# A sliding-window copy: two pairs of windows and three small DMAs placed among the software ring's DMAs

## The chip, the cores and the metric

The kernel runs on one core of a Trainium2 chip. A core has five engines that execute instructions (here only three of them issue anything: SP, ACT and POOL) and 16 DMA engines that move bytes between the chip's memory (HBM) and the core's on-chip memory (SBUF), or from HBM to HBM. The time is the device time of one execution in microseconds (us). Before the change the median of 3 runs was 743.77 us (742.8 to 744.65).

## The reference

```python
batch, length, dim = (32, 4096, 256)      # x, float32
window_size = 64; stride = 32
n_windows = (length - window_size) // stride + 1      # 127
for i in range(n_windows):
    start = i * stride
    result[:, i] = x[:, start:start + window_size].copy()
```

Nothing is computed. For each of 32 batches the output holds 127 windows of 64 rows of 256 numbers. A window is 64 KB; two neighbours overlap by half, so each block of 32 rows (32 KB) of the input goes to two windows, once as a second half and once as a first half.

## The kernel before, in words

The kernel only issues DMAs, on three queues, and no data passes through a compute engine.

- ACT's queue (the staged batches, lines 49 to 123): 11 of the 32 batches, 1, 4, 7 and so on up to 31, are loaded into SBUF (128 blocks of 32 KB, one to a partition) and stored from there twice, once as first halves and once as second halves. There are six buffers, and a semaphore `stored0` to `stored5` for each of them counts the stores.
- SP's queue (the direct batches, lines 175 to 190): the other 21 batches are copied from HBM to HBM, 16 windows at a time. Some of these are split into the two halves of the windows. The variables `turns` and `share` choose how the two hardware queues are paced against each other.
- POOL's queue (lines 192 to 201): the rest of the direct batches. POOL's DMAs are written by software into a ring of descriptors, which is why its queue is called the software ring here. It waits for the semaphore `near`, which the last but one 16-window copy of SP raises, and then issues 20 copies of 15 windows each (the list `edges`, one for each direct batch but the last). Before each copy it waits until the staged batches next to it have been stored. Then come one copy of 4 windows of batch 30 (`last`), its windows 112 to 115, and one copy `columns` of the nine windows 116 to 124.

`windows` (line 29) issues a copy of n windows of 64 KB. In the instruction each window is one row of two pieces of 32 KB, so its form is n x 2 x 8192 elements. `columns` (line 40) cuts each window into 16 parts of 4 KB and makes the part the outer count, so its form is 16 x n x 1024. SP issues the last two windows of batch 30 in the same way at line 203, when the last staged batch has been stored; then it waits for all semaphores at line 206. POOL issues `drain` (line 201) after its last copy.

Of the kernel before, what the change touches and what calls it, by code (L numbers as in the profile page):

```python
# [11 lines left out]
class Copier:  # L12
# [7 lines left out]
        self.nb = L // S  # L20
        self.nw = n_win

    def xap(self, block, dims):
        return bass.AP(self.x.tensor, self.x.offset + block * self.blk, dims)

    def oap(self, half_window, dims):
        return bass.AP(self.out.tensor, self.out.offset + half_window * self.blk, dims)

    def windows(self, q, b, w0, n, half=None, piece=DIRECT):

# [9 lines left out]
    def columns(self, q, b, w0, n):  # L40

        part = self.blk // 8
        row = [1, part]
        return q.dma_start(  # L44
            out=self.oap((b * self.nw + w0) * 2, [[part, 16], [2 * self.blk, n], row]),
            in_=self.xap(b * self.nb + w0, [[part, 16], [self.blk, n], row]),
        )

    def load(self, q, t, b, c, rows):
# [76 lines left out]
@with_exitstack  # L126
def kernel(
    ctx: ExitStack,
    tc: tile.TileContext,
    x: bass.AP,  # L130
    window_size: bass.AP,
    stride: bass.AP,
    out: bass.AP,
):
    nc = tc.nc
    W, S = int(window_size), int(stride)
    B, L, D = x.shape
    n_win = (L - W) // S + 1
    assert out.shape == (B, n_win, W, D)
    c = Copier(x, out, B, L, D, W, S, n_win)  # L140


    staged = [*range(1, B, 3)]
    items = [(b, -1 if b == B - 1 else 0, c.nb) for b in staged]
    place = {b: g for g, (b, _, n) in enumerate(items) if n == c.nb}
    direct = [b for b in range(B) if b not in staged]
    pool = ctx.enter_context(tc.tile_pool(name="xb", bufs=1))
    st = Staging(c, tc, pool, x.dtype, items, 6)
    ring_d, ring_s, ring_r = nc.sync, nc.scalar, nc.gpsimd
    done = tc.alloc_semaphore("done")  # L150
    near = tc.alloc_semaphore("near")
    rest = tc.alloc_semaphore("rest")
    total = {done: 0, near: 0, rest: 0}

    def count(dma, sem):
        dma.then_inc(sem, 16)
        total[sem] += 16

    sixteens = []
    for b in direct:
        w = 15 if b - 1 in staged else 0
        sixteens += [(b, w + 16 * j) for j in range((c.nw - w) // 16)]
    singles = [(B - 1, c.nw - 1, 1)]
    edges = [(b, 0 if b - 1 in staged else 112, 15) for b in direct[:-1]]
    last = B - 2
    edges.append((last, 112, 4))

    first_loads, loads, stores = 6 * 17, 5 * 17, 6 * 34  # L170
    turns = share = 0
    with tc.tile_critical():  # L172
        st.run(ring_s)

        for i, (b, w) in enumerate(sixteens):
            sem = near if i == len(sixteens) - 2 else done
            second = turns - first_loads - stores
            loading = turns < first_loads or 0 <= second < loads
            share += 120 if turns < 16 or -8 <= second < 16 else 90 if loading else 18
            if share >= 120:  # L180
                share -= 120
                turns += 4
                count(c.windows(ring_d, b, w, 16, 0), done)
                count(c.windows(ring_d, b, w, 16, 1), sem)
            else:
                turns += 3
                count(c.windows(ring_d, b, w, 16), sem)
            if i == len(sixteens) // 2:
                for b, w, half in singles:
                    count(c.windows(ring_d, b, w, 1, half, 2048), done)  # L190

        ring_r.wait_ge(near, 16)
        for b, w, n in edges:
            for k in (b - 1, b + 1):
                if k in place and b != last:
                    st.wait_stored(ring_r, place[k])
            count(c.windows(ring_r, b, w, n), rest)


        count(c.columns(ring_r, last, 116, 9), rest)  # L200
        ring_r.drain()  # L201
        st.wait_stored(ring_d, place[B - 1])
        count(c.columns(ring_d, last, 125, 2), done)
        total[st.ended] = st.count[st.ended]
        for sem, n in total.items():
            ring_d.wait_ge(sem, n)
# [35 lines left out]
```

## Time and profile before

| | |
|---|---|
| median of 3 runs | 743.77 us (742.8 to 744.65) |
| the profiled execution | 743.86 us |
| its span, first to last instruction | 742.1 us |
| SP's queue (q1) | 8016 packets, 154.32 MB |
| ACT's queue (q10) | 9104 packets, 138.41 MB |
| POOL's queue (q0) | 1168 packets, 20.51 MB |
| POOL starts its copies at | 649.11 us |
| POOL waits for a store from, for | 659.36 us, 36.49 us |
| POOL's last copy is issued at | 697.85 us |
| SP's last copy is issued at | 723.77 us |

The page gives the busy share of the 16 DMA engines in 40 slices of the span, the bytes that each of them moved, and the DMA queues by their packets. Another view gives the same shares in any stretch of the span, and one more follows the chain of waits that ended last. The trace also holds a record of each packet, with its start, its duration, its queue and its size, though not with the DMA engine that moved it.

### The profile page before, as it was taken

What the parts mean: (1) busy time and instruction counts of PE and PEld (TensorE: products, weight loads), DVE (VectorE), ACT (ScalarE), POOL (GpSimd) and SP (SyncE); (2) the same over time, 40 slices, a digit from 0 to 9 for tenths busy, and PEclk for the clock granted to TensorE, in tenths of its full rate; (3) what the DMA queues carried; (4) which work ended last, traced back from release to release, by engine and by line L of the source; (5) the groups of instructions that cost most, each with busy time, mean ns of one, the idle gap of its engine ahead of it and who ended that gap; (6) DMA issues with size and microseconds to landing.
All of it is one profiled execution on the core that took longest, in us unless ns stands there. A gap on an engine that the chain in (4) does not pass through costs nothing.

```text
span 742.1 us, 323 instructions
## 1 busy us (share of the span) xinstructions
POOL 12.7 (2%) x26
## 2 busy tenths in 40 slices
POOL 0000000000000000000000000000000000050100
DMA  8999999999999999999999999999999999999996
GB/s 361 424 430 427 435 431 428 423 435 425 428 427 426 428 428 420 429 435 427 427 427 412 433 435 431 427 436 432 434 424 429 430 424 426 428 435 432 421 420 253
DMA packets 18290, 313.26 MB, mean 422 GB/s; under 512 B 4336, under 2 KB 4336, under 8 KB 4528
## 3 DMA queue, kind: packets, MB, share of 16 engines
q1 hardware_dynamic: 8016, 154.32, 48.8%
q10 hardware_dynamic: 9104, 138.41, 44.0%
q0 software_dynamic: 1168, 20.51, 6.6%
q14 instruction: 2, 0.02, 0.0%
HBM read 220.95 MB, written 267.09 MB: 658 GB/s over the span
## 4 chain that ended last, share of the span: by engine, by line
another core or an unknown queue 92%; POOL 2%; issue 0%; POOLq 0%; SPq 0%
POOL out_dram L34 2%; POOLq L201 0%; POOLq L237 0%; SPq L172 0%; POOLq L114 0%
## 5 line engine op out<-in xcount | busy, mean ns | idle before, releaser
L34 POOL DMA_DIRECT2D out_dram<-in_x_dram x21 | 12.0, 575 | 685.4 <-DMA out_dram<-in_x_dram 648.7
L44 POOL DMA_DIRECT2D out_dram<-in_x_dram x1 | 0.6, 581 | 0.0
L223 POOL MEMSET const-float32-0.0<- 128x1 f32 x1 | 0.1, 98 | 0.2 <-issue 0.2
L223 POOL MEMSET const-bfloat16-1.0<- 128x1 bf16 x1 | 0.1, 101 | 0.0
L223 POOL MEMSET const-float32-1.0<- 128x1 f32 x1 | 0.1, 98 | 0.0
L223 POOL MEMSET const-uint8-127<- 128x1 uint8 x1 | 0.1, 98 | 0.0
## 6 DMA issues: line engine op xcount, KB each, us to landing
out_dram<-in_x_dram SPq DMA_DIRECT2D x92, 1024.0 KB, 99.8
out_dram<-xb ACTq DMA_DIRECT2D x21, 4096.0 KB, 138.5
out_dram<-in_x_dram SPq DMA_DIRECT2D x110, 512.0 KB, 90.2
xb<-in_x_dram ACTq DMA_DIRECT2D x10, 4096.0 KB, 130.5
out_dram<-in_x_dram POOLq DMA_DIRECT2D x20, 960.0 KB, 37.9
xb<-in_x_dram ACTq DMA_DIRECT2D x4, 1024.0 KB, 15.7
out_dram<-xb ACTq DMA_DIRECT2D x2, 1024.0 KB, 110.5
out_dram<-xb ACTq DMA_DIRECT2D x4, 512.0 KB, 94.4
```

Source lines behind the costliest of these rows:

```text
L34: return q.dma_start(out=self.oap((b * self.nw + w0) * 2 + h, [[2 * blk, n], row]), in_=self.xap(b * self.nb + w0 + h, [[blk, n], row]), m ...
L44: return q.dma_start(out=self.oap((b * self.nw + w0) * 2, [[part, 16], [2 * self.blk, n], row]), in_=self.xap(b * self.nb + w0, [[part, 16 ...
L223: nc = _bacc.Bacc("TRN2", target_bir_lowering=False, num_devices=1)
```

## The change

The software ring issues 26 DMAs instead of 22. The 4-window copy of batch 30 becomes two copies of 2 windows, one before the 17th of the 15-window copies and one before the 20th. Behind each of them stands a small new DMA, `pieces`: window 116 of the same batch is cut into 64 parts of 1 KB, and the even ones of these are copied, 6 parts by the first small DMA (`first` 0, `n` 3, two parts for each count of n) and 26 parts by the second (`first` 3, `n` 13). The last `columns` copy has eight windows instead of nine, and a new DMA `odd` behind it copies the 32 odd parts of window 116. The words by which the change was described say that its DMAs are reordered with four small ones between them so that one certain DMA engine gets one row of 64 KB less and another one more. What SP and ACT issue stays the same.

```diff
+    def pieces(self, q, b, w, first, n):
+
+        part = self.blk // 32
+        dims = [[4 * part, n], [2 * part, 2], [1, part]]
+        return q.dma_start(
+            out=self.oap((b * self.nw + w) * 2, dims, first * 4 * part),
+            in_=self.xap(b * self.nb + w, dims, first * 4 * part),
+        )
+
+    def odd(self, q, b, w):
+
+        part = self.blk // 32
+        dims = [[2 * part, 32], [1, part]]
+        return q.dma_start(
+            out=self.oap((b * self.nw + w) * 2, dims, part),
+            in_=self.xap(b * self.nb + w, dims, part),
+        )
...
     last = B - 2
-    edges.append((last, 112, 4))
...
         ring_r.wait_ge(near, 16)
-        for b, w, n in edges:
+        row = 116
+        for i, (b, w, n) in enumerate(edges):
+            if i == 16:
+                count(c.windows(ring_r, last, 112, 2), rest)
+                count(c.pieces(ring_r, last, row, 0, 3), rest)
+            if i == 19:
+                count(c.windows(ring_r, last, 114, 2), rest)
+                count(c.pieces(ring_r, last, row, 3, 13), rest)
             for k in (b - 1, b + 1):
-                if k in place and b != last:
+                if k in place:
                     st.wait_stored(ring_r, place[k])
             count(c.windows(ring_r, b, w, n), rest)
 
 
-        count(c.columns(ring_r, last, 116, 9), rest)
+        count(c.columns(ring_r, last, row + 1, 8), rest)
+        count(c.odd(ring_r, last, row), rest)
         ring_r.drain()
```

`xap` and `oap` get an argument `extra`, an offset in elements, that the new functions use. `self.blk` is 8192 elements, so `part` is 256 elements, 1 KB.

More of the change, by code (lines that the diff above doesn't have):

```diff
@@ L21, in __init__, with xap, oap @@
         self.nw = n_win
[L23 to L27, printed above, removed]
+    def xap(self, block, dims, extra=0):
+        return bass.AP(self.x.tensor, self.x.offset + block * self.blk + extra, dims)
+    def oap(self, half_window, dims, extra=0):
+        return bass.AP(self.out.tensor, self.out.offset + half_window * self.blk + extra, dims)
     def windows(self, q, b, w0, n, half=None, piece=DIRECT):
```

## The prediction

> **What bounds the kernel now.** I read the page first, then short windows at the end of the span, then the waits of SP's queue, then the packet records of the trace. The page:
>
> ```profile
> span 742.1 us, 323 instructions
> ...
> DMA  8999999999999999999999999999999999999996
> GB/s 361 424 430 427 435 431 428 423 435 425 428 427 426 428 428 420 429 435 427 427 427 412 433 435 431 427 436 432 434 424 429 430 424 426 428 435 432 421 420 253
> ...
> q1 hardware_dynamic: 8016, 154.32, 48.8%
> q10 hardware_dynamic: 9104, 138.41, 44.0%
> q0 software_dynamic: 1168, 20.51, 6.6%
> ...
> out_dram<-in_x_dram POOLq DMA_DIRECT2D x20, 960.0 KB, 37.9
> ...
> out_dram<-in_x_dram POOLq DMA_DIRECT2D x1, 576.0 KB, 42.3
> out_dram<-in_x_dram POOLq DMA_DIRECT2D x1, 256.0 KB, 38.0
> ```
>
> The reader is to see that nothing computes, that the 16 DMA engines are busy in every slice but the first and the last, and that the software ring (q0, 22 DMAs issued by POOL) carries only 20.51 of 313.26 MB. So the bytes set the time, and the only slack left is how evenly the 16 engines end. One microsecond at a time, with the columns stretch, its length, POOL, clock, DMA share and GB/s:
>
> ```profile
> 733.00:734.00 1.00, 0.00 (x0) 1.00 0.83 340
> 734.00:735.00 1.00, 0.00 (x0) 1.00 0.73 299
> 735.00:736.00 1.00, 0.00 (x0) 1.00 0.41 168
> 736.00:737.00 1.00, 0.00 (x0) 1.00 0.11 45
> 737.00:738.00 1.00, 0.00 (x0) 1.00 0.07 29
> 738.00:739.00 1.00, 0.00 (x0) 1.00 0.06 25
> 739.00:740.00 1.00, 0.00 (x0) 1.00 0.04 16
> ```
>
> A share of 0.06 is one engine in sixteen. From 737 to past 739 one engine works alone. SP waits for exactly that:
>
> ```profile
> SPq L206 <- DMA out_dram<-in_x_dram: 15.8, 1, 15.8
> ```
>
> The packet records give start, duration, queue and bytes, but no engine. On one engine a packet starts 3 to 6 ns before the last one's end, and the order of sizes on each queue is known from the program, so the 18,288 packets of the three data queues fall into 16 sequences of 19.578 MB each, all of them saturated from 2.8 us on (the latest one has 0.30 us of gaps). In the software queue each sequence has 38 packets of 32 KB, that is 19 rows of 64 KB, and 9 of 4 KB. Every 15-window DMA leaves out exactly one sequence, each a different one for 16 DMAs, and DMAs 17 to 20 leave out again the first four; those four get the rows of the 4-window DMA. So the ring deals rows in turn and goes on where the last DMA stopped: 20 x 15 + 4 = 304 = 16 x 19. I number the engines by it: the first DMA leaves out engine 15, the next 14, and so on. Where each engine's last packet ends, us from the span's start:
>
> ```
> engine   0      1      2      3      4      5      6      7
> end   735.77 734.14 734.86 735.20 739.70 734.26 735.11 734.94
> engine   8      9     10     11     12     13     14     15
> end   736.09 735.16 734.61 735.91 736.15 735.27 735.57 737.23
> ```
>
> Engine 4 ends 2.47 us after the next one. Its packets are only a little slower (16 KB: 622 ns on average against 615 to 620), and its lag behind the median engine, in bytes at 27 GB/s (32 KB in 1213 ns), grows through the whole span: 1.0 us at 69, 2.0 at 429, 3.3 at 609. After 739.70 comes the last count at 740.14 and the close until 742.09, 2.39 us together. The profiled execution took 743.86 us, 1.76 beyond its span and 0.09 above the median of 743.77.
>
> **What the change would be worth if the deal moved as described.** After 16 DMAs of 15 windows all engines have 15 rows and the next share is engine 0's. Two rows go to engines 0 and 1. A small DMA then moves the place by p, three 15-window DMAs follow, two rows, a small DMA that moves it by q, and the last 15-window DMA. With p = 3 and q = 13 the three DMAs leave out 4, 3 and 2, the two rows go to 2 and 3, the last leaves out 0: engine 4 has 18 rows, engine 1 has 20, the others 19. A row is two packets of 1245 ns on engine 4: 2.49 us, less two overlaps of 4 ns, 2.48. Engine 4 would end at 737.2, engine 1 at 734.14 + 2.48 = 736.6, and engine 15, untouched, at 737.2. Gain 2.4.
>
> **Why I don't take it.** The small DMA is written as n pieces of two steps, 3 x 2 x 256 elements, but the second step is 512 elements and the first 1024, so the two steps are one: the built program carries 6 x 256 and 26 x 256, with one counting step. A DMA that deals by its outer count has 6 and 26 to deal, never 3 and 13. The software ring of before has no copy with one counting step (its forms are 15 x 2, 4 x 2 and 16 x 9), so what the ring does with 6 and 26 has to be bounded:
> - It spreads them over all engines and does not move the place (p = q = 0): the 15-window DMAs leave out 1, 0, 15 and 0, the pairs go to 0, 1 and 15, 0. Sum: every engine 19 rows.
> - It moves by 6 and by 26, that is 10: engine 7 has 18, engine 1 has 20.
> - It moves by 6 and by 13, the largest count up to 16 that divides 26: engines 3 and 7 have 18, 0 and 1 have 20; engine 0 ends at 738.3.
>
> In all three engine 4 keeps its 19 rows and ends last. I take the first, because the hardware ring's one-step form, 16 x 8192, falls on all 16 engines in the records; but the sum is the same in each.
>
> The Trainium skill (DMA: Bandwidth & Descriptors, Why a DMA increments its semaphore by 16 and not by 1) says that the share count is the largest number up to 16 that divides the slowest counting step, but that the software ring gives some direct copies all 16 engines, and that the place moves only for fewer than 16. The 15 and 4 shares of this trace agree with its first half; no row here shows the exception. By the rule it would be 6 and 13, by the exception no move: 743.9 by either.
>
> **The rest of the change, on engine 4.** One 4 KB packet less: its group takes 159 ns, 156 from start to start. The window 116 comes instead as 64 pieces of 1 KB, 4 to an engine on average; I take 5 on engine 4. None of that size is in the trace; the 16 packets of 2 KB took 84 ns each, the 4-byte ones 9. A line through 84 and 159 gives 46 ns: 5 x 46 = 0.23 us, with ends 5 x 9 and 6 x 84, 0.05 to 0.50. Four more DMAs add a 4-byte packet each, three where the engine has no data (as its records show for the DMA that leaves it out), 6 ns from start to start: 0.02 to 0.07. Sum: -0.16 + 0.23 + 0.04 = +0.1, ends -0.1 and +0.4.
>
> **Off the path.** POOL issues 26 DMAs instead of 22, 575 to 581 ns each: 2.3 us more in all. The chain of waits has its last stretch
>
> ```profile
> 649.11 10.25 POOL out_dram L34 x18
> 659.36 36.49 another core or an unknown queue
> 695.85 0.28 issue
> 696.14 1.72 POOL out_dram L34 x3
> 697.85 0.58 POOLq L201
> ```
>
> The first pair and its pieces go ahead of the 36.5 us wait, the second pair, its pieces and the odd pieces behind it, so the last issue moves from 697.85 to at most 700.2. At 697.85 every engine still has 8 to 9 rows of 64 KB queued, and the first packet of the 4 KB columns starts at 732.74: more than 30 us of cover. If it were gone, each issue would cost its 0.58 us. No wait is added; the same 20 DMAs wait for the same stores, in the same order, and SP and ACT issue what they did. That two rows come earlier on engines 0 and 1 changes no end, since all are saturated. The close could grow with the number of DMAs that POOL drains: 26/22 of the 1.95 us after the last count would be +0.35, and I take nothing.
>
> Sum: 743.77 + 0.1 = **743.9 us**.
>
> **Rivals.**
> - *The place moves by 3 and 13 after all.* For: engine 4 is the one that ends last and engine 1 the one that ends first, so the numbers fit this trace exactly. Against: the instruction carries 6 and 26. Time: 743.77 - 2.48 + 0.1 = 741.4; engine 15 at 737.2 holds it from going lower.
> - *Slower: the place is carried from one execution to the next.* Before, 304 shares bring it back to where it began. With moves of 6 and 13 the sum is 323, 3 beyond 320, so each execution begins 3 engines on, and the pair of engines with 20 rows walks around. It decides where the pair holds engine 4 (2 executions in 16): 739.70 + 2.48 + 0.1 = 742.3, time 746.3. On engine 15 it would give 739.8, nothing. For: the place survives from DMA to DMA. Against: it needs the division rule, and then a bad place in most of the timed runs.
> - *Nothing is late for long:* engine 4's lag is this execution's alone. Then neither relief nor load shows, and the time lies within the runs' spread of 742.8 to 744.65.
>
> **Chances.** Within 0.3%, 2.2 us, is about what a measurement of this kernel can tell from no change. Engine 4 keeps 19 rows, with no extra row on it: 0.64, and its own range is 742.6 to 745.2 (the -0.1 and +0.75 of the bounds beside the runs' 0.9). Moved by 3 and 13: 0.24; its 2.4 us is just over the bound, so I count 0.14 of it as faster. Slower by carrying: 0.06. Something not named: 0.06. The third rival ends where the first case does and is counted in it. Faster 0.20 (with 0.03 from spread and 0.03 unnamed), slower 0.10 (0.04, 0.03, 0.03), same 0.70. The range has to reach the second case: 740.9 to 745.4.
>
> **What would show it.** In the trace after, the software queue should again have 38 packets of 32 KB in every one of the 16 sequences, 64 packets of 1 KB, 128 of 4 KB, and the same lone engine (share 0.06) for about 2.4 us before the end. The issue records should show element counts of 6 and 26 for the pieces. I am wrong if the engine that ends last has 36 packets of 32 KB (the first rival) or 40 (the second), or if the stretch with a share of 0.06 is gone.

## The result, and the profile after

The changed kernel took 745.38 us (median of 12 runs, 743.98 to 748.8) against 744.01 for the kernel before (12 runs, 742.8 to 745.61): a ratio of 1.0022, 95% interval 1.0013 to 1.0031. (The ratios here are those on record; they are not quotients of the two medians, which would give 1.0018.) It is 1.4 us slower, where 0.1 was forecast. The profiled execution took 746.16 us, more than the median by 0.8.

The page of the changed kernel:

```profile
span 744.4 us, 327 instructions
...
DMA  8999999999999999999999999999999999999995
...
q1 hardware_dynamic: 8016, 154.32, 48.8%
q10 hardware_dynamic: 9104, 138.41, 43.8%
q0 software_dynamic: 1296, 20.51, 6.6%
```

The bytes are the same; the software queue has 128 packets more (1168 before). The chain of waits, its last stretch:

```profile
650.54 9.64 POOL out_dram L34 x17
660.18 0.53 POOL out_dram L53
660.71 1.15 POOL out_dram L34 x2
661.86 35.50 another core or an unknown queue
697.37 0.28 issue
697.64 1.11 POOL out_dram L34 x2
698.75 0.55 POOL out_dram L53
699.31 0.56 POOL out_dram L34
699.87 0.55 POOL out_dram L44
700.42 0.53 POOLq L226
```

The last issue starts at 700.4 and ends at 700.95. That is 0.2 us past the bound of 700.2, because the wait for a store ended 1.5 us later in this execution (697.37 instead of 695.85), and it is still far from the end. The microseconds near the end (columns: stretch, length, POOL, clock, DMA share, GB/s) and SP's last wait:

```profile
735.00:736.00 1.00, 0.00 (x0) 1.00 0.66 268
736.00:737.00 1.00, 0.00 (x0) 1.00 0.46 182
737.00:738.00 1.00, 0.00 (x0) 1.00 0.24 100
738.00:739.00 1.00, 0.00 (x0) 1.00 0.01 2
739.00:740.00 1.00, 0.00 (x0) 1.00 0.08 33
740.00:741.00 1.00, 0.00 (x0) 1.00 0.05 20
741.00:742.00 1.00, 0.00 (x0) 1.00 0.04 14
```

```profile
SPq L231 <- DMA out_dram<-in_x_dram: 19.5, 1, 19.5
```

One engine is alone again, now up to 741.7: one engine of 16 busy is a share of about 0.06, and the stretches scatter around that. Laid out into 16 sequences, the packet records say that the deal did not move as described: every engine has 38 packets of 32 KB, 19 rows. The pieces of the 6 x 256 DMA lie on six engines one by one, and those of 26 x 256 on all 16, two on ten of them and one on six. Two pieces on one engine are one packet of 2 KB, so the records hold 12 packets of 1 KB and 26 of 2 KB where 64 of 1 KB were forecast. After both, the next copy goes on where the last pair of windows stopped. Engine 4 ends last, at 741.72; the next one is engine 2 at 738.12, and engine 1 ends first, at 735.03. So the rows lie as forecast, and the same engine is alone at the end, though for 3.6 us where about 2.4 were forecast. What differs most is the time.

Two stretches show where it is not, and where it is. By 650 us, before the software queue has moved a byte, this execution is already 0.41 MB behind the other one, 1.0 us at the 426 GB/s that both run at there. That is spread between executions: SP and ACT issue the same DMAs till then, and the profiles of `pairs` and `end` below, whose ratios are 0.9999 and 1.0006, are further behind at 649 us (275.64 MB each, 275.97 here, 276.41 before). From 729 us on, the view of the DMA queues in that stretch, first before and then after:

```profile
DMA packets 368, 2.53 MB, mean 158 GB/s; under 512 B 131, under 2 KB 131, under 8 KB 285
...
q0 software_dynamic: 256, 1.67, 26.0%
q10 hardware_dynamic: 86, 0.82, 12.6%
```

```profile
DMA packets 407, 2.85 MB, mean 178 GB/s; under 512 B 164, under 2 KB 170, under 8 KB 325
...
q0 software_dynamic: 349, 2.42, 40.1%
q10 hardware_dynamic: 46, 0.43, 7.0%
```

The software queue's rows (q0) have been left to the end, 2.42 MB instead of 1.67, and ACT's stores (q10) have gone ahead of them, 0.43 MB left instead of 0.82 (26 packets of 16 KB instead of 50). Of packets of 32 KB in the software queue 33 start after 729 us before, 56 after the change; those that start between 729 and 734 take 1302 ns on average before and 1430 after.

### The profile page after: what moved, and what is told of

Same layout as the page of the kernel before. It is cut to its first block, busy times and chain, and to the rows that moved or that the text cites. A ratio compares the mean times of both kernels' runs of the same rounds, so it can differ in the third digit from the quotient of the medians.

```text
span 744.4 us, 327 instructions
## 1 busy us (share of the span) xinstructions
POOL 14.8 (2%) x30
## 4 chain that ended last, share of the span: by engine, by line
another core or an unknown queue 92%; POOL 2%; issue 0%; POOLq 0%; SPq 0%
POOL out_dram L34 2%; POOL out_dram L53 0%; POOL out_dram L44 0%; POOLq L226 0%; POOLq L262 0%; SPq L189 0%; POOLq L132 0%
## 5 line engine op out<-in xcount | busy, mean ns | idle before, releaser
L34 POOL DMA_DIRECT2D out_dram<-in_x_dram x22 | 12.5, 573 | 685.9 <-DMA out_dram<-in_x_dram 650.1
L53 POOL DMA_DIRECT2D out_dram<-in_x_dram x2 | 1.1, 549 | 0.0
L44 POOL DMA_DIRECT2D out_dram<-in_x_dram x1 | 0.6, 554 | 0.0
L62 POOL DMA_DIRECT2D out_dram<-in_x_dram x1 | 0.5, 534 | 0.0
```

The costliest lines, as they stand in the source:

```text
L34: return q.dma_start(out=self.oap((b * self.nw + w0) * 2 + h, [[2 * blk, n], row]), in_=self.xap(b * self.nb + w0 + h, [[blk, n], row]), m ...
L44: return q.dma_start(out=self.oap((b * self.nw + w0) * 2, [[part, 16], [2 * self.blk, n], row]), in_=self.xap(b * self.nb + w0, [[part, 16 ...
L53: return q.dma_start(out=self.oap((b * self.nw + w) * 2, dims, first * 4 * part), in_=self.xap(b * self.nb + w, dims, first * 4 * part),)
L62: return q.dma_start(out=self.oap((b * self.nw + w) * 2, dims, part), in_=self.xap(b * self.nb + w, dims, part),)
```

## The experiments

The runs came in five groups. Ratios are always to the kernel before in the same group; its medians were 744.07, 744.19, 753.80, 751.32 and 743.79 us. Why two groups are slower is not on record: the chip numbered 9 stands for 744.19 as well as for 751.32.

**What two medians of the same program differ by, and the changed kernel again.** The first is the kernel before, unchanged.

> The kernel of before, unchanged, measured against itself, to see what two medians of the same program differ by. Every theory expects 744.0 us and a ratio of 1.000, with at most 0.1% of difference (0.7 us).

Measured: 743.49 us, ratio 0.9992 (0.9984 to 1.0001). So 0.1% between two medians says little by itself, and the changed kernel was measured three times more.

> The changed kernel a second time. Its profiled execution ended 2.3 us later than the one of before, and 1.0 us of that was behind in bytes moved by 660 us, when POOL had only just begun. Theory A (what the edit costs is its own work at the end: 0.1 us of small packets on engine 4 and 0.2 us of longer drain; the rest is spread between executions): 744.2 to 744.5 us here, ratio 1.0005. Theory B (something in the reordered ring costs more than its packets): 745.4 us again, ratio 1.002, and the lag in bytes at 660 us gone or halved in this profile. Both expect 19 rows of 64 KB on every engine and engine 4 last.

> The changed kernel a third time, on the same chip as the three others. Theory P and E: 1.002 again, 745.5 us; engine 4 last with 19 rows; more packets over 330 ns too long after 700 us than before had (4), as in its first two profiles (18 and 14).

> The changed kernel once more, on one chip with the next three. Theory T (turns ahead of the last rows): ratio 1.0015, and about 50 halves of rows, if it is the faster chip, after 729 us. If the earlier two medians were spread: 1.0004.

Measured: 1.0020 (1.0009 to 1.0030), 1.0005 (0.9991 to 1.0019), 1.0012 (0.9998 to 1.0026, in a slower group). With the first result, each weighted by its interval, that is 1.0017 with 0.0006 to either side: 1.3 us. The three repeats alone give 1.0014 with 0.0007. So the loss is clear of noise and somewhat smaller than in the first result.

**One part alone.** First the pairs without the small DMAs, then the small ones without the pairs:

```diff
             if i == 16:
                 count(c.windows(ring_r, last, 112, 2), rest)
-                count(c.pieces(ring_r, last, row, 0, 3), rest)
...
-        count(c.columns(ring_r, last, row + 1, 8), rest)
-        count(c.odd(ring_r, last, row), rest)
+        count(c.columns(ring_r, last, row, 9), rest)
```

> Only the two pairs of windows are moved ahead of the 17th and the 20th copy; no small DMAs, nine columns as before, 23 DMAs. 19 rows on every engine. Theory A: 744.0 to 744.2 us, as before. Theory B, if the earlier pairs are what costs: 745.4; if the small pieces are: 744.0.

```diff
             if i == 16:
-                count(c.windows(ring_r, last, 112, 2), rest)
                 count(c.pieces(ring_r, last, row, 0, 3), rest)
...
+        count(c.windows(ring_r, last, 112, 4), rest)
         count(c.columns(ring_r, last, row + 1, 8), rest)
```

> Only the small pieces: 6 x 256 before the 17th copy, 26 x 256 before the 20th, 32 x 256 at the end; the four windows stay one copy at the end, as before. 25 DMAs, 19 rows on every engine. So far the changed kernel measured 1.002 of before twice and the pairs alone 1.000. Theory P (small pieces in the middle of the ring cost, by slow packets around 718 to 726 us where the first of them ran): 1.002, 745.5 us, and a cluster of packets over 330 ns too long at that time. Theory D (what costs is the number of DMAs and the end): 1.0005 to 1.001.

Measured: pairs 0.9999 (0.9989 to 1.0009), small 0.9998 (0.9989 to 1.0008). Neither part costs by itself what both cost together. So small pieces in the middle of the ring do not cost it by themselves, as theory P had it.

**Pieces at the end, and many DMAs.** Window 116 in 1 KB pieces behind the columns; and the nine columns split over five DMAs:

```diff
+        count(c.windows(ring_r, last, 112, 4), rest)
         count(c.columns(ring_r, last, row + 1, 8), rest)
+        count(c.pieces(ring_r, last, row, 0, 16), rest)
         count(c.odd(ring_r, last, row), rest)
```

> Order of before, but window 116 goes as two DMAs of 32 pieces of 1 KB behind the columns, none in the middle. 24 DMAs. Theory P: 1.000 to 1.0005, no cluster at 718 to 726, and from the last packet to the span's end at most 0.3 us more than before (2.39 us). Theory E (1 KB pieces cost wherever they are): 1.002.

```diff
+        count(c.windows(ring_r, last, 112, 4), rest)
+        for w in range(116, 124, 2):
+            count(c.columns(ring_r, last, w, 2), rest)
+        count(c.columns(ring_r, last, 124, 1), rest)
```

> Order of before, the nine columns split over five DMAs, so 26 DMAs and no 1 KB piece. Theory D: from the last packet to the end 0.16 us more for POOL's drain, which grew from 0.50 to 0.66 us with 22 to 26 DMAs, and a ratio of 1.0003. If the number of DMAs is the whole cost: 1.002. Theory P: 1.000 to 1.0003.

Measured: end 1.0006 (0.9996 to 1.0015), many 1.0001 (0.9991 to 1.0012). The profiles give the price of a DMA in POOL's drain: from the last count of the software ring to the span's end it is 1.94 and 1.95 us with 22 DMAs, 1.99 with 23, 2.03 with 24, 2.06 with 25, 2.10 to 2.11 with 26. That is 0.04 us for each. With pieces of 1 KB as the last DMA the count itself also comes later after the last packet: 0.55 us in the changed kernel's first profile instead of 0.44, and 0.44 to 0.71 in the profiles of the other kernels that end so. So the close is 0.27 us longer in the changed kernel, and neither the number of DMAs (theory D) nor the 1 KB pieces by themselves (theory E) explains more than that.

**Turns.** The records of one engine show what a small packet costs its queue. In the kernel before, a copy that leaves an engine out still puts three packets of 4 bytes on it. Every copy also ends with one packet of 4 bytes on an engine that has its data. On engine 4 four packets of 4 bytes, the one that ends a copy and the three of the copy that leaves the engine out, start at 699.26, 699.87, 700.48 and 701.10 us: each is moved in 9 ns, and then the queue waits while a store of ACT's has its turn. The queues change at nearly every packet there, whatever its size. In the changed kernel an engine has about ten such packets more ahead of its last rows: three for each pair of windows it isn't part of, two for each small DMA. With the pairs alone there are six, with the small DMAs alone four. These are the turns of the table.

```
from 729 us on, faster groups    turns  q0 32 KB packets   ns of those that   16 KB stores
                                 ahead  starting            start 729-734     starting
before / control                   0      33 / 25           1302 / 1230        50 / 60
many / end                         0      39 / 34           1288 / 1224        65 / 82
small                              4      40                1343               46
pairs                              6      47                1264               62
changed, again, again2            10      56, 55, 48        1430, 1344, 1359   26, 29, 28
moves of 3 and 13 (below)         10      53                1410               29
turns behind the rows (late3)      0      34                1246               67
the row with two turns (shift2b)   2      43                1260               57
```

The column of packets follows the turns, and the slow rows come where fewest stores are left beside them. These are not yet the loss: `pairs` has 47 packets left and a ratio of 0.9999, and the profiled execution of `again2` has 48 and took 743.74 us.

A second count holds in all five groups and does not hang on a moment such as 729 us: the packets that start after 700 us and take over 330 ns longer than is usual for their size (1213 ns for 32 KB, 611 for 16 KB, 159 for 4 KB). Each profile is one execution.

```
turns ahead   profiles                                                    long packets
0             before, control, many, end, late, late2, late3              4 3 5 2 7 2 6
2             shift2, shift2b                                             3 5
4, 6          small; pairs                                                8; 8
10            after, again, again2, again3, near, deal, deal2, dealnear   18 14 18 13 21 12 27 22
16            turns                                                       32
```

In the kernels with ten turns many of those up to about 729 us come in groups of two to four, stores as well as rows, on some of the engines, which lose 1 to 4 us each. `many`, without turns, has one such group too (2.4 us on one engine), so the turns make the groups more frequent and are not their only source.

To test the order, the same 26 DMAs in the same forms, with the pairs and the small ones behind the twentieth copy:

```diff
-            if i == 16:
-                count(c.windows(ring_r, last, 112, 2), rest)
...
+        count(c.windows(ring_r, last, 112, 2), rest)
+        count(c.pieces(ring_r, last, row, 0, 3), rest)
+        count(c.windows(ring_r, last, 114, 2), rest)
+        count(c.pieces(ring_r, last, row, 3, 13), rest)
         count(c.columns(ring_r, last, row + 1, 8), rest)
```

> The 26 DMAs of the changed kernel in the same forms, but the two pairs and the two small DMAs stand behind the twentieth 15-window copy. Each engine has 19 rows either way. Theory T (turns): on an engine the queues take turns packet by packet, and in the changed kernel an engine has about ten 4-byte and 1 KB packets of the software queue ahead of its last rows (before: none of them); each gives a store of 611 ns the turn, so rows are left to the end, where they run without stores beside them and take 1340 to 1430 ns instead of 1290. Then with the turns behind the rows there should be about 33 rows after 729 us (before 33, changed 48 to 56) at 1230 to 1300 ns, and what is left is 0.3 us of longer close: ratio 1.0004, 744.4 us. Theory D (26 DMAs, or small pieces anywhere): 1.0015.

> The same 26 DMAs with the pairs and small ones behind the rows. Theory T: 1.0004 (0.3 us of longer close), and 0.8 us or 0.1% under the changed kernel beside it. If small DMAs cost wherever they stand: as the changed kernel.

> Theory T: 1.0004, as the mean of its first two (1.0000 and 1.0010). If small DMAs cost wherever they stand: 1.0015.

Measured: 1.0000 (0.9988 to 1.0012), 1.0010 (0.9997 to 1.0023), 1.0006 (0.9997 to 1.0015); together 1.0005 with 0.0006 to either side, 0.4 us. The third ran in a group as fast as the first result's, and in its last stretch, from 729 us, the software queue has as much left as in the kernel before (1.70 MB against 1.67), and ACT's stores are not ahead of it:

```profile
DMA packets 525, 2.85 MB, mean 178 GB/s; under 512 B 247, under 2 KB 259, under 8 KB 424
...
q0 software_dynamic: 387, 1.70, 26.2%
q10 hardware_dynamic: 111, 1.10, 16.4%
```

34 packets of 32 KB start there, those up to 734 us at 1246 ns. Of the 0.4 us the longer close is 0.27; the rest is within the interval. Against the changed kernel's 1.0017 that is 0.0012 less, with some 0.0009 to either side, an interval that just leaves out zero; with the three repeats alone (1.0014) it would not, and in the one group that has both, `again3` and `late2` measured 1.0012 and 1.0010. And more turns, the even pieces of window 116 in eight DMAs of 4 x 256, four ahead of the 17th and four ahead of the 20th copy:

```diff
+            if i == 16 or i == 19:
+                for k in range(4):
+                    count(c.pieces(ring_r, last, row, 2 * k + 8 * (i == 19), 2), rest)
...
+        count(c.windows(ring_r, last, 112, 4), rest)
         count(c.columns(ring_r, last, row + 1, 8), rest)
```

> Four windows at the end as before, and the even pieces of window 116 in eight DMAs of 4 x 256, four ahead of the 17th copy and four ahead of the 20th: 16 turns ahead of the last rows instead of 10, and 31 DMAs. Theory T: 60 to 70 rows of 64 KB halves after 729 us at 1400 ns or more, few stores left there, ratio 1.002 to 1.003 (0.4 us of it a longer close). Theory D, with 0.04 us for each DMA: 1.0006.

Measured: 757.76 us, 1.0057 (1.0036 to 1.0079), 4.3 us. The close takes 2.31 us after the last count here (31 DMAs), 0.4 more than before. The rest, clear of noise, is put down to the order; the same 31 DMAs with the small ones behind the rows were not measured, so that their number alone costs nothing more is taken from `many` and `late`. In this slower group the last stretch, from 739 us, first with 16 turns ahead and then with the turns behind the rows:

```profile
q0 software_dynamic: 430, 2.53, 34.3%
q10 hardware_dynamic: 57, 0.56, 7.3%
```

```profile
q0 software_dynamic: 386, 1.67, 21.9%
q10 hardware_dynamic: 99, 0.95, 12.0%
```

As many rows are left as expected: 60 packets of 32 KB start after 739 us, against 33 with the turns behind. They took 1322 ns on average against 1232, less than the 1400 expected, and earlier, between 729 and 734 us, they were no slower (1257 ns against 1259). The slow packets there were ACT's stores: 52 took 895 ns on average, where the kernel with the turns behind has 40 at 664. So which queue's packets pay differs.

**POOL one copy earlier**, the changed kernel otherwise:

```diff
-            sem = near if i == len(sixteens) - 2 else done
+            sem = near if i == len(sixteens) - 3 else done
```

> The changed kernel, with the semaphore that POOL waits for raised one 16-window copy earlier, so that the software ring starts some 4 to 5 us earlier and its rows are done earlier. Theory T: fewer rows than 40 after 729 us, ratio 1.0005 or a little less. Theory D: 1.0015, as without it.

Measured: 1.0013 (0.9998 to 1.0028): not told apart from the changed kernel, and nothing follows. In this group, too, engine 4 ended last, at 750.71, but the next one at 749.34.

**The deal as it was described.** The pieces are taken from both halves of window 116, so that the steps can't be joined:

```diff
-        dims = [[4 * part, n], [2 * part, 2], [1, part]]
+        dims = [[part, n], [32 * part, 2], [1, part]]
...
-        count(c.odd(ring_r, last, row), rest)
+        count(c.pieces(ring_r, last, row, 16, 16), rest)
```

> The small DMAs take their pieces from both halves of window 116, so that their two steps cannot be joined and the instruction carries 3 x 2 and 13 x 2; the last one is 16 x 2. Theory of the place: now the deal moves by 3 and 13, engine 4 has 18 rows (36 packets of 32 KB), engine 1 has 20, all others 19. Engine 4 then ends 2.4 us earlier, level with the next ones: 2.0 to 2.4 us under the changed kernel, which is 742.0 to 743.3 us. Rival (the place does not move with small pieces either): 19 rows everywhere and the time of the changed kernel, 745.4.

> Moves of 3 and 13, engine 4 with 18 rows and ten turns ahead of the last rows. Theory T: the turns cost 0.8 us and the longer close 0.3, so of the 2.4 us about 1.3 should be left: ratio 0.998 to 0.999. If engine 4 loses as much by the order as it gains by the row, as in the first measurement: 1.000 to 1.001.

> The kernel whose deal moves by 3 and 13 (engine 4 has 18 rows), and POOL starts one copy earlier. If the delayed rows took the gain of that deal (it measured 1.001 where 2.4 us less, 0.997, was expected): 742.2 to 743.0 us, ratio 0.9975 to 0.9990, with engine 4 level with engines 8, 12 and 15. If engine 4's lag has another cause that grows with this order: 1.000 to 1.001.

Measured: 1.0010 (0.9999 to 1.0021), 1.0021 (1.0006 to 1.0036), and with POOL earlier 1.0006 (0.9992 to 1.0020). The first profile confirms the theory of the place: engine 4 has 18 rows, engine 1 has 20, the others 19. The time does not follow. Engine 4 still ends last in this profile of `deal`, at 740.38, 1.75 us after engine 12, as the same view shows (a share of 0.07 from 738.6 on):

```profile
737.00:738.00 1.00, 0.00 (x0) 1.00 0.21 86
738.00:739.00 1.00, 0.00 (x0) 1.00 0.07 29
739.00:740.00 1.00, 0.00 (x0) 1.00 0.07 29
740.00:741.00 1.00, 0.00 (x0) 1.00 0.02 6
```

On engine 4 three stores between 721.4 and 725.7 us took 1109, 1087 and 2095 ns instead of 611: 2.5 us, as much as the row. In the second profile of the changed kernel the same engine lost 3.4 us in four packets from 719 to 726 us and ended at 743.58. In the kernel before no engine had such a group there. Both have the ten turns. In the profiles of `deal2` and `dealnear` engine 4 is no longer last (in `dealnear` another one is, by 2.0 us), and the time is no better: the slow packets fall on other engines too.

**The row taken with two turns.** With `pieces` again taken from both halves: one small DMA of 2 x 2 pieces ahead of the 13th copy, the rest of the window behind the columns. Engines 4 and 5 then have 18 rows, 0 and 1 have 20:

```diff
+            if i == 12:
+                count(c.pieces(ring_r, last, row, 0, 2), rest)
...
+        count(c.windows(ring_r, last, 112, 4), rest)
         count(c.columns(ring_r, last, row + 1, 8), rest)
         count(c.pieces(ring_r, last, row, 16, 16), rest)
+        count(c.pieces(ring_r, last, row, 2, 14), rest)
```

> One small DMA of 2 x 2 pieces ahead of the 13th copy, and 16 x 2 and 14 x 2 behind the columns; the four windows stay at the end. The place moves by 2 between the 12th and 13th copy, so engines 4 and 5 have 18 rows, 0 and 1 have 20, the others 19, with two turns ahead of the rows instead of ten. Theory T: engine 4 ends 2.4 us earlier, engine 0 at 738.3 and 15 at 737.3 set the end: 0.3 us of close and 0.2 of turns beside it, ratio 0.9978 to 0.9988, below before and all others. If the row is not worth its 2.4 us: 1.000.

> Engines 4 and 5 with 18 rows. If engine 4's lead at the end is the bound and the row counts for its size: on the faster chip (744 us) 0.9978 to 0.9988, on a slower one (751 or more) 0.9990 to 1.0000. If other engines or engine 4's slow packets fill the place: 1.0004 again.

Measured: 1.0004 (0.9991 to 1.0016) in a slower group, 0.9990 (0.9979 to 1.0000) in a fast one, 743.23 us. In both profiles engine 0, now with 20 rows, ends last: by 1.4 us in the first, by 0.7 in the second, the shortest lone stretch but two of all these profiles (0.4 in `again3`, 0.2 in `deal2`):

```profile
736.00:737.00 1.00, 0.00 (x0) 1.00 0.43 174
737.00:738.00 1.00, 0.00 (x0) 1.00 0.32 127
738.00:739.00 1.00, 0.00 (x0) 1.00 0.09 33
739.00:740.00 1.00, 0.00 (x0) 1.00 0.00 0
```

It is under the kernel before by 0.1% at best, which is as much as the unchanged kernel differed from itself: no version was found that is measurably faster.

## Why the prediction was right or wrong

- **The steps join, and engine 4 keeps its 19 rows:** right, and by the first of the three cases. The issue records show 6 and 26 pieces, no engine has 36 or 40 packets of 32 KB, and the same engine ends alone.
- **The small packets' own time on engine 4, +0.1 us:** nothing contradicts it; a piece of 1 KB took 46 to 47 ns, as estimated, and the kernels with 1 KB pieces behind the rows cost 0.4 us together, of which 0.27 is the close.
- **The close, taken as unchanged with +0.35 as a bound:** mis-sized. It measured +0.27: 0.16 in the drain (0.04 for each DMA) and 0.11 until the last count.
- **"That two rows come earlier on engines 0 and 1 changes no end, since all are saturated", and the 4-byte packets at 6 ns from start to start:** this is the step that failed. The engines are saturated, and a 4-byte packet does take 9 ns, but it uses up a turn of its queue: 0.61 us where a store waits, not 6 ns. The sum priced the four more DMAs by the bytes and records they add, 0.02 to 0.07 us, and their place ahead of the last rows at nothing. In its place the runs show this. The rows are left to the end, with fewer stores beside them: 26 of these start after 729 us instead of 50, so more were let ahead, though far fewer than ten on each engine. And 12 to 27 packets are much too long after 700 us, against 2 to 7 where at most two turns stand ahead. The same DMAs behind the rows measured 1.0005 and the changed kernel 1.0017; the difference of 0.9 us (0.0012, with some 0.0009 to either side) is the best figure for the price of the order, and a loose one. Neither half shows it alone: the earlier pairs measured 0.9999 and the small DMAs 0.9998. More turns, 1.0057, point the same way.
- **The chances and the range:** 745.38 lies at the upper edge of the range, and that it lies inside is luck: the bounds were made of the close and the small packets' own time, not of the order. The first case's own range, 742.6 to 745.2, is not what the bounds named beside it add up to (742.8 to 745.4 from 743.77). The difference is real but under the 0.3% that was taken as a measurement's limit; 12 runs told 0.2% apart.
- **The rival of 3 and 13, 741.4 us:** the deal can be made to move so, and the relief is of the size expected in rows, but the time was 1.0010 and 1.0021. The 2.4 us were read from one execution's lone engine; the lone stretch measures 0.2 to 4.9 us in the twenty profiles. What takes the gain is seen in one profile (stores of nearly twice the usual time and more on engine 4, in the order with ten turns) and not shown in general. That leaves open how much of a row's time a relief of engine 4 brings.
- **The rival of the carried place:** its condition was not met, since the small DMAs don't move the place.
- **The rival that engine 4's lag is one execution's alone:** wrong. The unchanged kernel run again (`control`) has engine 4 last too, by 1.9 us.

Left open is also what makes engine 4 the last in nearly every execution with 19 rows on it, in faster and slower groups, and by what mechanism single packets take much longer, and rows at the end somewhat longer, when small packets go ahead of the rows.

## What to carry to other kernels

Where several queues share an engine, count packets, not only bytes: in this kernel a copy that leaves an engine out, or a very small DMA, takes a turn there and moves what is behind it back, and the same small DMAs came out cheaper behind the large ones. Look at the form that the built instruction carries before counting on how a copy is spread: two steps that join are one. And a lone engine at the end of one profile is worth what several profiles agree on, not what one shows.

## What the runs showed of the hardware that was not expected

- A software-ring copy with one counting step is dealt over all 16 engines and leaves the place as it was: 6 pieces one by one on six engines, 26 as two on ten and one on six (the changed kernel). With two counting steps it is dealt by the outer count, 3, 13, 2 or 14 as well as 15 and 4, and moves the place by it (`deal`, `shift2b`).
- An engine without data in such a copy still gets packets: three of 4 bytes for a copy of windows, two for a small one of one counting step; in a small one of two counting steps, one of 8 and one of 4 bytes.
- A packet of 4 bytes of the software queue delays its next packet by 0.61 us while stores of 16 KB wait in another queue.
- With ten or more such turns ahead of the last rows, 12 to 32 packets after 700 us take over 330 ns too long; with none to two, 2 to 7.
- POOL's drain at the end takes 0.04 us more for each DMA that it issued (1.94 us with 22, 2.31 with 31, from the last count to the end).
- With 19 rows on it the engine numbered 4 here ends last in 12 of the 15 profiles, by 0.8 (`pairs`) to 4.9 us (`again`), though not in `again3`, where engine 14 does, with two slow packets (2.0 us) at 728 to 732 us. In `end` and `turns` the records leave open which engine it is.
